# A hybrid attention, state-space and expert layer: a later DRAM copy, a seventh place for expert weights, products that run one pair later, and independent row stores

## The chip, the core and the metric

The kernel runs on one core of one Trainium2 chip. The metric is the time of one execution on the device, in microseconds (us). The program is written with a tile framework: it traces the operations in the order of the source, places the tiles, orders each engine's queue and sets the waits. Engines are PE (matrix multiply; PEld is its weight load), DVE (vector), ACT (activation), POOL (general), and SP, which here only issues DMAs. DMAs are also issued from the queues of ACT and POOL.

## The reference, cut to what matters

512 tokens of width 1024, with 16 learned tokens in front, go through a norm and one wide projection. From it come a latent attention of 16 heads and a state-space scan of 16 heads; both are gated, merged, projected and added to the input. Then follows a mixture of experts: each token chooses one of 4 groups and two of the 8 experts in it.

```
u = rmsnorm(h, norm_mix);  proj = u @ w_in
o_attn = mla_branch(...);  o_ssm = ssd_branch(...)
h = h + (sigmoid(g_attn) * (o_attn @ w_branch_attn)
         + sigmoid(g_ssm) * (o_ssm @ w_branch_ssm)) @ w_out
v = rmsnorm(h, norm_ffn)
for gi in range(4):          # experts of group gi
    hid = silu(v @ w_gate[e]) * (v @ w_up[e])
    out = out + comb[:, e] * (hid @ w_down[e])
return rmsnorm(h + out, norm_final)[16:]
```

An expert has 2 MB of gate and up weights and 1 MB of down weights; 32 experts make 96 MB.

## The kernel before, in words

**Start.** The rows of x are loaded in blocks of 128 (`load_x`), normed and transposed into a split pair `uh`, `ul`. Inside one `in_order` block the queues of ACT, DVE, POOL, PE and SP keep the order of the source: `u_rstd(4)` (line 188) needs the last 16 rows, tile `xm` (line 160), and stands on ACT ahead of the scaling (line 207) that the transposes of block 2 on PE (line 212) need.

**Row buffer.** `vd` is a DRAM buffer of 1024 rows of 1025 words. Its lower 512 rows get the output of the first half of the layer with a scale in the last word (lines 1158 and 1190); the expert stage gathers its token rows from there. The upper 512 rows are a copy of x, with one word more per row (lines 948 and 949): a stand-in that the expert stage's overflow code writes over. The copy depends on nothing, so the framework is free to put its two DMAs anywhere on SP's queue.

**Attention.** In the part around line 950, `load_w` loads the chunks of `wbs` (line 225); `prep` sends rows of the rotated queries to the tiles `qs` by small DMAs on SP (line 798); `find_max` (line 809) multiplies `qs` by `kq` on PE, tile `sp`.

**Routing.** Each token's experts are chosen, and with one-hot products each expert gets a list of up to 64 rows. If an expert had more, `tc.If(over > 0)` (line 1431) would run a slow loop; on these inputs its body does not run, but every engine passes the branch. On the false side SP's queue waits until every DMA that was issued on it has landed.

**Expert stage.** 16 pairs of experts, one expert on each half of the partitions. A pair p does:

```
expert_gu(p)             # gate and up, tanh, products: gu, th, hp
load_gu(...)             # next weights into the places just read
turn_x(p + 1)            # transposes of the next pair's rows (pxT)
combine(p - 1, 1, (0,))  # one-hot product (pc), a quarter
expert_h(p)              # transposes of hp (phT), copy hT by ACT
combine(p - 1, 1, (1,))
y_start; y_mm; y_split   # down product y, split into yh, yl
combine(p, 0)            # two quarters of this pair's one-hot products
```

All this is inside `in_order(act, dve, pe, pool, nc.sync)`, so each queue keeps the order of the source. `combine` adds a pair's rows, for column half hh and row block b, into one of four PSUM sums; after four pairs `add`, `norm` and `scale` (lines 1630 to 1640) finish a group's rows, which `group_rows` gathered into the tiles `res`, and `put_rows` (line 1426) stores them by an indirect DMA on POOL. The framework treats two such stores as writes to the same output, so the second waits until the first has landed. `group_tables` (lines 1598 to 1600) builds on DVE the one-hot tables from which `group_places` (line 1607, PE) finds the group lists; it stands in pair 0 behind the transposes of pair 1.

**Places.** Gate and up weights of expert e lie in place e % 6 (`GU_AT`), down weights in place e % 7. Experts 0 to 5 are loaded as memory comes free, experts 2p + 6 and 2p + 7 (line 1037) when pair p has read its own; line 1046 loads the down weights. The tile `h2`, which holds the output of the first half, is dead once its rows are in `vd`; its memory (tag "v") is then `fin`: two row buffers `res` and the final gain, which is loaded at line 1423. `fence` (line 1488) is a small DMA that SP issues when POOL has issued the first three gathers; down weights 5 and 6 are queued behind it.

Of the kernel before, what the change touches and what calls it, by code (L numbers as in the profile page):

```python
# [9 lines left out]
F32 = mybir.dt.float32  # L10
# [5 lines left out]
ALU = mybir.AluOpType  # L16
# [3 lines left out]
T = 512  # L20
NM = 16
L = T + NM
D = 1024
# [49 lines left out]
def hybrid_layer(ctx: ExitStack, tc, A, out):  # L73
    nc = tc.nc
# [872 lines left out]
    vd = drp.tile([2 * T, D + 1], F32, name="vd")  # L947
    nc.sync.dma_start(vd[T:, :D], A["x"])
    nc.sync.dma_start(vd[T:, D:], A["x"][:, :1])
    PP, pos, l8s, lis = {}, {}, {}, {}  # L950
# [68 lines left out]

    GU_AT = "uu" + "0" + "a" + "d" + "b"  # L1020
    DN_AT = "0aadcee"

    def load_gu(e, parts=(0, 1)):

        if e >= NE:
            return
        i = e % NR
        w = GU_AT[i]
        if i in gus:
            pass  # L1030
        elif w == "u":
            gus[i] = btile(f"gu{i}", n=T)
        else:
            gus[i] = mws[w].tile([128, 4096], F32, tag=f"gu{i}", name=f"gu{i}", bufs=1).rearrange("p (k n) -> p k n", k=KD)
        for h in parts:
            k = slice(h * 4, h * 4 + 4)
            nc.sync.dma_start(gus[i][:, k], A["moe_gu"][e].rearrange("p (k n) -> p k n", k=KD)[:, k])
# [298 lines left out]
    with in_order(pe):  # L1336
# [5 lines left out]
        mws["d"] = ctx.enter_context(tc.tile_pool(name="mwd", bufs=1, reuse_waits="tile", side="right"))  # L1342
        load_gu(4)
        for i in range(3, ND):
# [52 lines left out]
    for x in xgs:  # L1397
        pool.memset(x, 0.0)
    load_gu(5)
    with tc.issue_after(last_rs[0].ins):  # L1400
        for i in range(3, ND):
            if DN_AT[i] == "c":
                load_dn(i)


    fin = btile("fin", n=T, tag="v").rearrange("p k n -> p (k n)")
    res, gfin = [fin[:, b * (D + 1):(b + 1) * (D + 1)] for b in range(2)], fin[:, 2 * D + 2:3 * D + 2]

# [6 lines left out]
    with in_order(pool):  # L1415
        for p in range(NX):
            gather(p)
        pool.memset(flag, 0.0)
        for x in res:
            pool.memset(x, 0.0)  # L1420
    iot = rx.tile([128, 360], F32, tag="rx", name="iot")[:, :GCAP]
    nc.sync.dma_start(iot, bcast_row(A["iota"], GCAP))
    nc.sync.dma_start(gfin, bcast_row(A["g_fin"], D))

    def put_rows(places, rows):
        nc.gpsimd.indirect_dma_start(out=out, out_offset=bass.IndirectOffsetOnAxis(ap=places, axis=0),
                                     in_=rows, in_offset=None, bounds_check=T - 1, oob_is_err=False)


    over = nc.values_load(ovi[0:1, 0:1], min_val=0, max_val=1)  # L1430
    with tc.If(over > 0), tc.tile_pool(name="fb", bufs=1, side="right") as fb:
        wrd = drp.tile([NE, 128, 4], F32, name="wrd")
        nc.sync.dma_start(wrd.rearrange("e p b -> p e b"), wrest)
        for b in range(4):
# [40 lines left out]

            yo = ev.tile([128, D], F32, tag="yl", name="yo", bufs=1)
            fs, fi = fb.tile([128, 2], F32, tag="fs", name="fs"), fb.tile([128, 1], I32, tag="fi", name="fi")
            act.activation(yo, acc, AF.Square, scale=D ** -0.5, accum_out=fs[:, 0:1])
            dve.tensor_scalar(fs[:, 1:2], fs[:, 0:1], EPS, None, op0=ALU.add)
            pool.tensor_tensor(fs[:, 1:2], fs[:, 1:2], mhalf[:, :1], op=ALU.pow)  # L1480
            dve.scalar_tensor_tensor(yo, acc, fs[:, 1:2], gfin, op0=ALU.mult, op1=ALU.mult)
            dve.scalar_tensor_tensor(fs[:, 0:1], gk[:, b:b + 1], GCAP - 0.5, tok1[:, b:b + 1], op0=ALU.is_gt, op1=ALU.mult)
# [3 lines left out]
    mws["e"] = ctx.enter_context(tc.tile_pool(name="mwe", bufs=1, reuse_waits="tile", side="right"))  # L1486
    fence = drp.tile([128, 1], F32, name="fence")
    with tc.issue_after(nc.sync.dma_start(fence, flag).ins):
        for i in range(3, ND):
            if DN_AT[i] == "e":  # L1490
                load_dn(i)

# [22 lines left out]
    def expert_gu(p):  # L1515

        nf = 1 if p < 15 else 2
        gu = [ps("gu") for _ in range(nf)]
        th, hp = (ev.tile([128, 256], F32, tag=x, name=x, bufs=n) for x, n in (("th", 1), ("hp", 2)))
        h_[p] = hp  # L1520
        n = 256 // nf
        for kh in range(2):
            for f in range(nf):
                for k in range(kh * 4, kh * 4 + 4):
                    for e in range(2):
                        r, w = slice(e * 64, (e + 1) * 64), gus[(2 * p + e) % NR][:, k]
                        if nf > 1:
                            w = w.rearrange("p (g f n) -> p g f n", g=2, f=nf)[:, :, f]
                        pe.matmul(gu[f][r, :2 * n], xT[p][:, k, r], w, start=(k == 0), stop=(k == KD - 1), skip_group_check=True)  # L1529
                if kh:  # L1530
                    c = slice(f * n, (f + 1) * n)
                    act.activation(th[:, c], gu[f][:, :n], AF.Tanh, scale=rsl[:, p:p + 1])  # L1532
                    dve.scalar_tensor_tensor(hp[:, c], th[:, c], 1.0, gu[f][:, :n], op0=ALU.add, op1=ALU.mult)  # L1533
                    dve.tensor_mul(hp[:, c], hp[:, c], gu[f][:, n:2 * n])
# [75 lines left out]
    def group_lists():  # L1610
# [6 lines left out]
        dve.tensor_add(gsrc, gw[:, :, 0], gw[:, :, 1])  # L1617

    def group_rows(g):
        for b in range(2):  # L1620
            nc.gpsimd.indirect_dma_start(out=res[b], out_offset=None, in_=vd,
                                         in_offset=bass.IndirectOffsetOnAxis(ap=gsrc[:, b, g:g + 1], axis=0),
                                         bounds_check=2 * T - 1, oob_is_err=False)
# [14 lines left out]
    def scale(g, b):  # L1638
        x = res[b][:, :D]
        dve.scalar_tensor_tensor(x, x, fq[:, 8 + b:9 + b], gfin, op0=ALU.mult, op1=ALU.mult)  # L1640
        put_rows(gdst[:, b, g:g + 1], x)
# [3 lines left out]
    with in_order(act, dve, pe, pool, nc.sync):  # L1645
        for hh in range(2):
            turn_x(0, hh)
        for p in range(16):
            g, last = p // 4, p % 4 == 3
            expert_gu(p)  # L1650
            for h in range(2):
                for e in range(2 * p + NR, 2 * p + NR + 2):
                    load_gu(e, (h,))
            if p < 15:
                turn_x(p + 1, 0)
                turn_x(p + 1, 1)
                if p == 0:
                    group_tables()
                if p:
                    combine(p - 1, 1, (0,))  # L1660
                expert_h(p)
                if p == 0:
                    group_places()
                if p:
                    combine(p - 1, 1, (1,))
                y_start(p)
                for hh in range(2):
# [3 lines left out]
                    if p and p % 4 == 0:  # L1671
                        add(hh, 1)
            else:
                y_start(p)
                expert_h(p, (0,))
                combine(p - 1, 1, (0,))
# [15 lines left out]
            if p < 15:  # L1692
                combine(p, 0)
            if last and p < 15:
                for b in range(2):
                    add(b, 0)
            if p and p % 4 == 0:
# [4 lines left out]
            if p % 4 == 2:  # L1702
                group_rows(g)
        for hh in range(2):
            for b in range(2):
                combine(15, hh, (b,))
                add(b, hh)
                if hh:
                    norm(b)
        for b in range(2):  # L1710
            scale(3, b)
# [117 lines left out]
```

## Time and profile before

| | |
|---|---|
| median of 3 runs | 840.69 us (840.56 to 842.31) |
| the profiled execution | 844.1 us |
| its span, first to last instruction | 842.3 us |
| PE busy in the span | 783.6 us (93%) |
| DVE, ACT, POOL busy | 441.7, 281.9, 162.6 us |
| moved by DMA | 167.58 MB |

The expert stage begins at about 589 us, when the first gathered rows have landed. The rows below give a start in us from the beginning of the span and a duration in us; the square bracket is the time that the engine sat idle before the row and what ended it.

### The profile page before, as it was taken

To read this page: it belongs to the slowest core of one execution; us is meant where nothing else is said; L and a number is where in the kernel's file an instruction comes from. 1 tells how busy PE (TensorE), PEld (TensorE's weight loads), DVE (VectorE), ACT (ScalarE), POOL (GpSimd) and SP (SyncE) were. 2 spreads that over 40 slices of the span, in tenths; PEclk is the share of its full clock that TensorE was granted. 3 is DMA by queue.
4 is the path that set the end of the run, shared out by engine and by line. 5 is a ranking of instruction groups with operands and counts; after the bars stand their busy time and mean duration, and the time that the engine had idled before them with its cause. 6 is when DMAs were issued, how large, how long until landed. Compare 5 with 4: busy or idle time off the path is not lost.

```text
span 842.3 us, 11392 instructions
## 1 busy us (share of the span) xinstructions
PE 783.6 (93%) x4202; PEld 531.0 (63%) x4202; DVE 441.7 (52%) x1005; ACT 281.9 (33%) x541; POOL 162.6 (19%) x222
## 2 busy tenths in 40 slices
PE   4799999999999999999999899995899999999992
PEld 3699988677778878876666588884333333333341
DVE  3487627886465445477774675435223433423423
ACT  4545524433234473155554233311111212212212
POOL 4200011333201000014444200007101121220202
PEclk9899999999999999999999999997799999999997
DMA  9322125234212215020112494586799999999970
GB/s 302 103 101 100 57 97 170 105 126 139 88 63 100 100 36 192 21 60 26 47 52 73 149 420 189 176 333 220 242 421 419 418 418 417 419 420 416 422 284 18
DMA packets 42573, 167.58 MB, mean 199 GB/s; under 512 B 10336, under 2 KB 14832, under 8 KB 26384
## 3 DMA queue, kind: packets, MB, share of 16 engines
q1 hardware_dynamic: 36560, 156.55, 48.8%
q0 software_dynamic: 5136, 10.04, 3.8%
q8 instruction: 35, 0.57, 0.3%
q14 instruction: 26, 0.21, 0.1%
q10 hardware_dynamic: 816, 0.20, 0.1%
HBM read 165.60 MB, written 8.45 MB: 207 GB/s over the span
## 4 chain that ended last, share of the span: by engine, by line
PE 81%; DMA 6%; DVE 6%; ACT 4%; issue 2%; POOL 0%; POOLq 0%; ACTq 0%; SPq 0%; DVEq 0%
PE gu L1529 14%; PE y L1562 7%; PE pbr L671 3%; PE pbr L669 3%; PE pbr L668 3%; PE po L871 2%; DMA xm<-in_x_dram 2%; PE pc L1583 2%; PE ga L241 2%; PE gs L241 2%; PE ga L243 2%; PE ga L242 2%; PE gs L242 2%; PE pout L1092 2%; PE gs L243 2%
## 5 line engine op out<-in xcount | busy, mean ns | idle before, releaser
L1529 PE MATMUL gu<-gu,xT 128*64 128x512 f32 (+1 forms) x544 | 115.5, 578 | 0.0
L1529 PEld LDWEIGHTS gu<-gu,xT 128*64 128x64 f32 x544 | 38.1, 139 | 69.6 <-issue 65.4
L1562 PE MATMUL y<-dn,hT 128*64 128x512 f32 x256 | 60.4, 614 | 0.9
L1533 DVE SCALAR_TENSOR_TENSOR hp<-th,gu 128x256 f32<-128x256 f32 (+1 forms) x17 | 6.9, 405 | 95.5 <-ACT th L1532 95.5
L1570 DVE SCALAR_TENSOR_TENSOR yl<-y,wsl,yh 128x512 fp32r<-128x512 f32 x30 | 22.5, 751 | 50.6 <-ACT yh L1569 49.6
L1532 ACT ACTIVATE th<-gu,rsl 128x256 f32<-128x256 f32 (+1 forms) x17 | 7.8, 461 | 114.7 <-PE gu L1529 114.7
L817 DVE CUSTOM_DVE_ANT_0 sp<-sp,amask 128x144 f32<-128x144 f32 (+4 forms) x80 | 33.9, 459 | 18.0 <-PE sp L809 15.9
L1562 PEld LDWEIGHTS y<-dn,hT 128*64 128x64 f32 x256 | 17.3, 139 | 35.7 <-issue 27.9
L1410 POOL DMA_INDIRECT xg<-vd,idx x16 | 16.4, 1028 | 116.9 <-issue 52.3
L1569 ACT ACTIVATE yh<-y,wsl 128x512 fp32r<-128x512 f32 x30 | 20.6, 685 | 47.1 <-PE y L1562 38.7
L847 PE MATMUL st<-qs,kq 97*128 97x512 f32 (+4 forms) x80 | 28.7, 358 | 1.0 <-DVE kq L792 1.0
L1583 PE MATMUL pc<-yh,st 128*128 128x512 f32 x60 | 27.7, 462 | 0.0
L301 POOL TENSOR_TENSOR rfs<-rfm,mhalf 128x4 f32<-128x4 f32 (+1 forms) x5 | 7.6, 1519 | 92.6 <-DVE rfm L300 92.6
L1503 PEld LDWEIGHTS pxT<-cst,xg 128*128 128x128 f32 x128 | 14.4, 146 | 17.5 <-issue 12.2
L877 POOL TENSOR_TENSOR pw<-pw 128x400 f32<-128x400 f32 x14 | 15.9, 1157 | 44.4 <-PE po L871 44.4
L1505 DVE TENSOR_TENSOR xT<-pxT,pv 128x512 f32<-128x512 f32 x32 | 20.6, 683 | 6.2 <-PE pxT L1503 6.1
L848 PE MATMUL st<-qs,kq 97*128 97x512 f32 (+4 forms) x80 | 23.6, 296 | 0.2 <-DMA qs<-rs 0.2
L1583 PE MATMUL pc<-yl,st 128*128 128x512 f32 x60 | 23.7, 396 | 0.0
L1503 PE MATMUL pxT<-cst,xg 128*128 128x128 f32 x128 | 18.3, 289 | 5.2 <-DMA xg<-vd,idx 5.2
L387 DVE SCALAR_TENSOR_TENSOR cacc<-xp,cwh,cacc 128x528 f32<-128x528 f32 x30 | 22.9, 763 | 0.4
L856 ACT ACTIVATE pw<-st 128x512 f32<-128x512 f32 (+1 forms) x32 | 16.7, 546 | 19.2 <-PE st L852 16.1
L849 PE MATMUL st<-qs,kq 97*128 97x512 f32 (+4 forms) x80 | 23.0, 294 | 0.0
(926 smaller groups left out, 2110.0 us busy)
## 6 DMA issues: line engine op xcount, KB each, us to landing
gu<-in_moe_gu_dram SPq DMA_DIRECT2D x64, 1024.0 KB
dn<-in_moe_dn_dram SPq DMA_DIRECT2D x30, 1024.0 KB
win<-in_win_dram SPq DMA_DIRECT2D x19, 1024.0 KB
lm<-acd SPq DMA_DIRECT2D x16, 256.0 KB
wbs<-in_wbs_dram SPq DMA_DIRECT2D x4, 1024.0 KB
wba<-in_wba_dram SPq DMA_DIRECT2D x4, 1024.0 KB
wo<-in_wout_dram SPq DMA_DIRECT2D x4, 1024.0 KB
vd<-in_x_dram SPq DMA_DIRECT2D x1, 2048.0 KB
```

What stands on the lines that cost most here:

```text
L241: pe.matmul(dst, ah, bh, start=(i == 0), stop=False)
L242: pe.matmul(dst, ah, bl, start=False, stop=False)
L243: pe.matmul(dst, al, bh, start=False, stop=(i == n - 1))
L668: pe.matmul(pb_, wh[:, k], oh[k], start=(k == 0), stop=False)
L669: pe.matmul(pb_, wh[:, k], ol[k], start=False, stop=False)
L671: pe.matmul(pb_, wl[:, k], oh[k], start=False, stop=(k == last))
L817: dve.tensor_tensor_reduce(s_, s_, amask[:, L - nk + n0:L - nk + n1], 1.0, -3.0e38, op0=ALU.add, op1=ALU.max, accum_out=mx[:, n_:n_ + 1])
L847: pe.matmul(d_, kh_[0:97, kb], qh_[0:97, q0:q1], start=True, stop=False)
L1503: pe.transpose(pt[:, k * 128:(k + 1) * 128], xgs[p % NX][:, (hh * 4 + k) * 128:(hh * 4 + k + 1) * 128], ident)
L1529: pe.matmul(gu[f][r, :2 * n], xT[p][:, k, r], w, start=(k == 0), stop=(k == KD - 1), skip_group_check=True)
L1562: pe.matmul(yp[hh][e * 64:(e + 1) * 64], hT_[p][:, f, e * 64:(e + 1) * 64], dns[(2 * p + e) % ND][:, f, hh * 512:(hh + 1) * 512], start=(f ...
L1583: pe.matmul(sums[b, hh], st[:, b * 128:(b + 1) * 128], x[:, c], start=(n == 0 and p % 4 == 0), stop=(n == 1 and p % 4 == 3), skip_group_ch ...
```

## The change

Four things are done. The copy of x into the upper half of `vd` is put behind the last `load_w` before it, which is the last chunk of `wbs`. Expert 4's gate and up weights get a seventh place of their own, in the memory of `h2`, and are loaded behind `fence`; experts 5 and 6 take the places that 4 and 5 had, and pair 2 starts one load instead of two; `fin` is made, and the gain loaded, at the end of pair 2, and the clearing of `res` on POOL is dropped. Of a pair's four one-hot products three run in the next pair, one of them ahead of `expert_h`; `group_tables` comes before pair 0, and the last group finishes block 1 before block 0. Stores of rows no longer wait for each other.

```diff
-    nc.sync.dma_start(vd[T:, :D], A["x"])
-    nc.sync.dma_start(vd[T:, D:], A["x"][:, :1])
+    with tc.issue_after(last_load[0].ins):
+        nc.sync.dma_start(vd[T:, :D], A["x"])
+        nc.sync.dma_start(vd[T:, D:], A["x"][:, :1])
...
-    GU_AT = "uu" + "0" + "a" + "d" + "b"
+    GU_AT = "uu" + "0" + "a" + "d" + "b" + "v"
+    EV = 4
+    def place_of(e):
+        return NR if e == EV else (e - (e > EV)) % NR
...
-        load_gu(4)
+        load_gu(5)
...
-    load_gu(5)
+    load_gu(6)
...
-    fin = btile("fin", n=T, tag="v").rearrange("p k n -> p (k n)")
-    res, gfin = [fin[:, b * (D + 1):(b + 1) * (D + 1)] for b in range(2)], fin[:, 2 * D + 2:3 * D + 2]
...
-        for x in res:
-            pool.memset(x, 0.0)
+    fence = drp.tile([128, 1], F32, name="fence")
+    with tc.issue_after(nc.sync.dma_start(fence, flag).ins):
+        load_gu(EV)
...
-    nc.sync.dma_start(gfin, bcast_row(A["g_fin"], D))
+    stores = []
     def put_rows(places, rows):
+        i = nc.gpsimd.indirect_dma_start(out=out, ...).ins
+        for j in stores:
+            tc.declare_no_dep(i, j, reason="rows of other tokens")
+        stores.append(i)
...
     mws["e"] = ctx.enter_context(tc.tile_pool(name="mwe", bufs=1, reuse_waits="tile", side="right"))
-    fence = drp.tile([128, 1], F32, name="fence")
-    with tc.issue_after(nc.sync.dma_start(fence, flag).ins):
-        for i in range(3, ND):
+    for i in range(3, ND):
...
     def group_rows(g):
+        if g == 0:
+            fin = btile("fin", n=T, tag="v").rearrange("p k n -> p (k n)")
+            res.extend([...])
+            nc.sync.dma_start(res[2], bcast_row(A["g_fin"], D))
...
+        group_tables()
         for p in range(16):
             expert_gu(p)
             for h in range(2):
-                for e in range(2 * p + NR, 2 * p + NR + 2):
-                    load_gu(e, (h,))
+                for e in (2 * p, 2 * p + 1):
+                    if e != EV:
+                        load_gu(e + NR + (e < EV), (h,))
             if p < 15:
                 turn_x(p + 1, 0)
                 turn_x(p + 1, 1)
-                if p == 0:
-                    group_tables()
                 if p:
+                    combine(p - 1, 0, (1,))
                     combine(p - 1, 1, (0,))
                 expert_h(p)
...
                     if p and p % 4 == 0:
-                        add(hh, 1)
+                        for b, h in ([(1, 1)] if hh else [(1, 0), (0, 1)]):
+                            add(b, h)
             else:
                 y_start(p)
+                combine(p - 1, 0, (1,))
                 expert_h(p, (0,))
...
-                combine(p, 0)
-            if last and p < 15:
-                for b in range(2):
-                    add(b, 0)
+                combine(p, 0, (0,))
+            if p % 4 == 3 and p < 15:
+                add(0, 0)
...
-        for hh in range(2):
-            for b in range(2):
+        for b in (1, 0):
+            for hh in range(2):
                 combine(15, hh, (b,))
                 add(b, hh)
-                if hh:
-                    norm(b)
-        for b in range(2):
+            norm(b)
             scale(3, b)
```

The overflow code loads the final gain for itself, since `fin` does not exist there any more; it does not run on these inputs.

## Rows read from the trace of the kernel before

**Rows 1.** The page: DMA share in 40 slices; the chain that ended last, by engine.

```profile
DMA  9322125234212215020112494586799999999970
...
PE 81%; DMA 6%; DVE 6%; ACT 4%; issue 2%; POOL 0%; POOLq 0%; ACTq 0%; SPq 0%; DVEq 0%
```

**Rows 2.** Timeline of SP's queue, first 12 us: start, duration, issue.

```profile
3.74 0.64 SPq L948 DMA_DIRECT2D vd<-in_x_dram  x1
...
5.34 6.51 SPq L160 DMA_DIRECT2D xm<-in_x_dram  x2
```

**Rows 3.** Windows at the start: busy us by engine, PE clock, DMA share, GB/s.

```profile
0.00:14.00 14.00, 4.01 (x16) 3.00 (x16) 4.77 (x11) 7.22 (x12) 6.21 (x12) 1.00 0.87 315
14.00:24.00 10.00, 5.68 (x25) 5.20 (x24) 2.70 (x4) 1.71 (x3) 3.18 (x6) 1.00 1.04 274
27.00:31.00 4.00, 3.98 (x19) 3.99 (x20) 2.45 (x2) 3.81 (x6) 3.50 (x12) 0.50 0.05 11
```

**Rows 4.** Timelines of ACT and PE at the start.

```profile
23.84 0.63 ACT L188 ACTIVATE junk<-xm 16x512 bf16<-16x512 f32 x1 [8.06 <-DMA xm<-in_x_dram]
...
19.41 1.91 PE L321 MATMUL first0a<-uh,win0l 128*128 128x256 f32 x8
27.02 1.97 PE L212 MATMUL pt<-cst,xin 128*128 128x128 f32 x8 [5.70 <-ACT xin L207]
```

**Rows 5.** SP's queue around 325 us; the products that read qs (min/median/max ns, first to last).

```profile
322.37 0.53 SPq L225 DMA_DIRECT2D wbs<-in_wbs_dram  x1
327.32 1.60 SPq L798 DMA_DIRECT2D qs<-rs  x2
...
L809 PE MATMUL sp<-kq,qs x80: 170/334/495, 344.2 to 445.7; 96*128 96x144 f32 x16, 96*128 96x272 f32 x16, 96*128 96x16 f32 x16, 96*128 96x400 f32 x16
```

**Rows 6.** Timeline of pair 0, from the copy of hT to the down product.

```profile
602.12 0.38 ACT L1545 ACTIVATE hT<-phT 128x256 f32<-128x256 f32 x1 [1.44 <-PE phT L1543]
...
604.30 0.34 PE L1607 MATMUL pg<-gtab,rrg 128*128 128x8 bf16 x8 [2.22 <-DVE gtab L1600]
...
604.58 5.35 PE L1562 MATMUL y<-dn,hT 128*64 128x512 f32 x16
```

**Rows 7.** Timeline of PE in a regular pair.

```profile
697.33 7.09 PE L1529 MATMUL gu<-gu,xT 128*64 128x512 f32 x32
...
706.07 0.41 PE L1543 MATMUL phT<-cst,hp 128*128 128x128 f32 x2 [0.17 <-DVE hp L1534]
...
707.01 3.65 PE L1562 MATMUL y<-dn,hT 128*64 128x512 f32 x16
...
711.74 7.09 PE L1529 MATMUL gu<-gu,xT 128*64 128x512 f32 x32
```

**Rows 8.** SP's queue at the branch.

```profile
588.45 0.34 SPq L1488 DMA_DIRECT2D fence<-flag  x1
597.78 1.01 SPq L1046 DMA_DIRECT2D dn<-in_moe_dn_dram  x2
```

**Rows 9.** Windows in the expert stage, columns as in rows 3.

```profile
588.00:594.00 6.00, 5.05 (x16) 2.58 (x18) 1.57 (x4) 0.00 (x0) 3.58 (x7) 0.50 0.34 69
610.00:800.00 190.00, 186.99 (x872) 73.26 (x874) 68.86 (x148) 37.70 (x77) 32.39 (x29) 1.00 1.02 419
812.00:818.00 6.00, 6.00 (x55) 3.83 (x55) 0.75 (x1) 0.18 (x2) 0.00 (x0) 1.00 0.57 212
818.00:820.00 2.00, 2.00 (x19) 1.16 (x15) 0.58 (x2) 0.69 (x3) 0.00 (x0) 1.00 0.04 15
```

**Rows 10.** Timelines of PE, DVE and POOL in the last 21 us.

```profile
821.57 2.79 PE L1562 MATMUL y<-dn,hT 128*64 128x512 f32 x12
...
831.83 1.29 DVE L1640 SCALAR_TENSOR_TENSOR fin<-fin,fq 128x1024 f32<-128x1024 f32 x1 [0.44 <-POOL fq L1636]
...
831.98 2.07 POOL L1426 DMA_INDIRECT out_dram<-fin,gdst  x1 [0.18 <-issue]
837.12 0.98 POOL L1426 DMA_INDIRECT out_dram<-fin,gdst  x1 [3.07 <-DMA out_dram<-fin,gdst]
```

More of the change, by code (lines that the diff above doesn't have):

```diff
@@ L1026, in load_gu @@
             return
-        i = e % NR
+        i = place_of(e)
         w = GU_AT[i]
@@ L1030, in load_gu @@
             pass
-        elif w == "u":
-            gus[i] = btile(f"gu{i}", n=T)
+        elif w in "uv":
+            gus[i] = btile(f"gu{i}", n=T, tag=w)
         else:
@@ L1418, in hybrid_layer @@
         pool.memset(flag, 0.0)
-        for x in res:
-            pool.memset(x, 0.0)
+    fence = drp.tile([128, 1], F32, name="fence")
+    with tc.issue_after(nc.sync.dma_start(fence, flag).ins):
+        load_gu(EV)
     iot = rx.tile([128, 360], F32, tag="rx", name="iot")[:, :GCAP]
     nc.sync.dma_start(iot, bcast_row(A["iota"], GCAP))
-    nc.sync.dma_start(gfin, bcast_row(A["g_fin"], D))
+    stores = []
     def put_rows(places, rows):
-        nc.gpsimd.indirect_dma_start(out=out, out_offset=bass.IndirectOffsetOnAxis(ap=places, axis=0),
-                                     in_=rows, in_offset=None, bounds_check=T - 1, oob_is_err=False)
+        i = nc.gpsimd.indirect_dma_start(out=out, out_offset=bass.IndirectOffsetOnAxis(ap=places, axis=0),
+                                         in_=rows, in_offset=None, bounds_check=T - 1, oob_is_err=False).ins
+        for j in stores:
+            tc.declare_no_dep(i, j, reason="rows of other tokens")
+        stores.append(i)
     over = nc.values_load(ovi[0:1, 0:1], min_val=0, max_val=1)
@@ L1474, in hybrid_layer @@
             nc.sync.dma_start(vd[T + b * 128:T + (b + 1) * 128, :D], acc)
-            yo = ev.tile([128, D], F32, tag="yl", name="yo", bufs=1)
+            yo, go = ev.tile([128, D], F32, tag="yl", name="yo", bufs=1), fb.tile([128, D], F32, tag="fw", name="go", bufs=3)
+            nc.sync.dma_start(go, bcast_row(A["g_fin"], D))
             fs, fi = fb.tile([128, 2], F32, tag="fs", name="fs"), fb.tile([128, 1], I32, tag="fi", name="fi")
@@ L1480, in hybrid_layer @@
             pool.tensor_tensor(fs[:, 1:2], fs[:, 1:2], mhalf[:, :1], op=ALU.pow)
[L1481 removed]
+            dve.scalar_tensor_tensor(yo, acc, fs[:, 1:2], go, op0=ALU.mult, op1=ALU.mult)
             dve.scalar_tensor_tensor(fs[:, 0:1], gk[:, b:b + 1], GCAP - 0.5, tok1[:, b:b + 1], op0=ALU.is_gt, op1=ALU.mult)
@@ L1486, in hybrid_layer @@
     mws["e"] = ctx.enter_context(tc.tile_pool(name="mwe", bufs=1, reuse_waits="tile", side="right"))
-    fence = drp.tile([128, 1], F32, name="fence")
-    with tc.issue_after(nc.sync.dma_start(fence, flag).ins):
-        for i in range(3, ND):
-            if DN_AT[i] == "e":
-                load_dn(i)
+    for i in range(3, ND):
+        if DN_AT[i] == "e":
+            load_dn(i)
     xT, h_, y_ = {}, {}, {}
@@ L1525, in expert_gu @@
                     for e in range(2):
-                        r, w = slice(e * 64, (e + 1) * 64), gus[(2 * p + e) % NR][:, k]
+                        r, w = slice(e * 64, (e + 1) * 64), gus[place_of(2 * p + e)][:, k]
                         if nf > 1:
@@ L1617, in group_lists @@
         dve.tensor_add(gsrc, gw[:, :, 0], gw[:, :, 1])
+    res = []
     def group_rows(g):
+        if g == 0:
+            fin = btile("fin", n=T, tag="v").rearrange("p k n -> p (k n)")
+            res.extend([*(fin[:, b * (D + 1):(b + 1) * (D + 1)] for b in range(2)), fin[:, 2 * D + 2:3 * D + 2]])
+            nc.sync.dma_start(res[2], bcast_row(A["g_fin"], D))
         for b in range(2):
@@ L1639, in scale @@
         x = res[b][:, :D]
-        dve.scalar_tensor_tensor(x, x, fq[:, 8 + b:9 + b], gfin, op0=ALU.mult, op1=ALU.mult)
+        dve.scalar_tensor_tensor(x, x, fq[:, 8 + b:9 + b], res[2], op0=ALU.mult, op1=ALU.mult)
         put_rows(gdst[:, b, g:g + 1], x)
@@ L1647, in hybrid_layer @@
             turn_x(0, hh)
+        group_tables()
         for p in range(16):
-            g, last = p // 4, p % 4 == 3
+            g = p // 4
             expert_gu(p)
             for h in range(2):
-                for e in range(2 * p + NR, 2 * p + NR + 2):
-                    load_gu(e, (h,))
+                for e in (2 * p, 2 * p + 1):
+                    if e != EV:
+                        load_gu(e + NR + (e < EV), (h,))
             if p < 15:
@@ L1663, in hybrid_layer @@
                     group_places()
-                if p:
+                else:
                     combine(p - 1, 1, (1,))
```

## The prediction

> **What bounds the kernel now.** I read the chain of waits first: PE carries 81% of it, and no other engine more than 6% [rows 1]. So a saving counts where PE sits idle or runs slowly, and at the two ends. The DMA line of the slices says where transfers may take over: it stands at 9 in the first slice and again from the thirtieth to the thirty-eighth, the expert stage [rows 1].
>
> The timelines then show the places. At the start PE ends its first product at 21.3 (19.41 + 1.91) and waits 5.70 us for ACT [rows 4]. ACT in turn waits 8.06 us for `xm`, until 23.84 [rows 4], though SP began to issue `xm` at 5.34 [rows 2]. In front of it on SP's queue stands the 2 MB copy of x, issued at 3.74 [rows 2]. [...] In pair 0 PE waits 2.22 us for the group tables, and the down product behind that wait takes 5.35 us [rows 6], where the same 16 matmuls take 3.65 us in a regular pair [rows 7]. A regular pair lasts 14.41 us (711.74 - 697.33), with one wait on its path, 0.17 us before the transposes of hp [rows 7]. At the end the second store waits 3.07 us for the first [rows 10].
>
> The sum is made against the profiled execution, 844.1 us (span 842.3, 1.8 around it); the median of the runs, 840.69, lies 3.4 us (0.4%) lower. About 0.2%, 1.7 us, is what a measurement of this kernel can tell from no change.
>
> **The change, part by part.**
>
> *The copy leaves the start: -8.0 us.* Ahead of `xm` remain 1.5 MB of x, 0.5 MB of gain, 0.1 MB of small loads and two chunks of 1 MB: with 1.05 MB to the chunk, 4.2 MB. At 315 GB/s the queues had moved 4.4 MB by 14 us [rows 3], so `xm` and the fourth block (0.5 MB, 1.6 us at that rate) would be in by about 16 to 17. From the arrival of `xm` to PE's next transpose ACT and POOL need 3.2 us (27.02 - 23.84) [rows 4]: 20.2, before PE ends its product at 21.3. So the whole 5.70 us goes. With no wait I expect no fall of the clock either: 4.0 us at 0.50 [rows 3] do 2.0 us of work, and with the shoulders of the slow stretch I take 2.3. Bounds: -5.0 if `xm` comes 2 us later than reckoned and the clock still falls in part, -8.5.
>
> *The copy in its new place: 0.* It brings two DMAs to SP's queue behind the chunk at 322.37 [rows 5]. Passed by it are the row DMAs `qs` at 327.32 [rows 5]. The copy took about 8 us of the DMA engines (2.1 MB at 274 GB/s) [rows 3]; behind 2.5 us of the chunk it would end near 334, the rows land a little later, and the first product that reads them starts at 344.2 [rows 5]. That slack of some 9 us is the cover; PE works on `wbs` meanwhile. Without cover it would cost up to 8 us and 2 us of slow clock. The column of 512 single words has no price of its own in the trace; in the first place both DMAs together fit between 14 and 24 [rows 3], so 10 us bounds the pair, and nothing suggests less than 0.
>
> *Group tables ahead of pair 0: -3.7 us.* Their six DVE operations move to where DVE idles while PE does the first gate product. The down product can then start when hT is copied, at 602.5 (602.12 + 0.38), plus some 0.06, instead of 604.58: 2.0 us [rows 6]. Kept warm, it takes 3.65 instead of 5.35: 1.7 us [rows 6, 7]. Bounds -2.0 and -4.2.
>
> *Products one pair later: -2.4 us.* PE does the same products; the one that moves ahead of the transposes of hp (two matmuls) fills the wait of 0.17 us [rows 7], in 14 pairs. Bounds: 0, if the wait only moves to hT, and -3.4, if the shorter block at the end of the pair saves another 0.07 each time.
>
> *Seventh place, fence and branch: +1.5 us.* The weights stream without a pause from about 598: DMA share 1.02 at 419 GB/s [rows 9]. A pair's 6 MB (6.29 million bytes) take 15.0 us at that rate, PE needs 14.41: the lead shrinks all the way. The stream drains between 812 and 818 [rows 9]; the last down weights are needed at 821.57 [rows 10]. So the slack is about 3.5 us, and it decides what the gains above are worth, since PE now comes 3.7 + 2.4 = 6.1 us earlier, at 815.5. The new place takes one expert's 2.1 MB (5.0 us) out of the stream and into the gap between 588 and 594, where only 69 GB/s are moved [rows 9]; the gain row (0.5 MB, 1.25 us) enters the stream: -3.75 us. Against that, SP must pass the branch. Between the fence at 588.45 and the first load behind the branch at 597.78 lie 9.3 us [rows 8]. Now two issues stand in between (0.8 us), and on the false side SP waits until they have landed, about 5 us, part of it beside the passage of the branch. Queued behind are down weights 5 and 6 and experts 7 and 8. I take 2.7 us of delay (bounds 0.8 and 5.3): the stream ends at 818 - 3.75 + 2.7 = 817.0, 1.5 us after the need. Bounds 0 and +4.0. The value lies nearer the lower, since the fence too had to land there.
>
> *Independent stores, last group by blocks: -2.6 us.* The second store starts at 837.12 though its rows were scaled at 833.1 (831.83 + 1.29) [rows 10]: 3.8 us with the 0.18 of issue. The new order gives back one scaling, 1.29 us, as the adds of block 0 stand on DVE behind the scaling of block 1. Bounds -1.0 and -3.8.
>
> *At nothing:* the dropped clearing of `res` and the gain's new issue (POOL and SP wait for nothing there), `fin` made at the end of pair 2, two pairs before its use, and the stores of the first three groups, behind which POOL's gathers have pairs of lead.
>
> Sum: -8.0 + 0 - 3.7 - 2.4 + 1.5 - 2.6 = -15.2 us: 828.9 for a profiled execution, **825.5 us** for the median.
>
> **The rivals.**
>
> *The branch holds the loads in full.* If SP passes the branch only after expert 4 has landed, the whole 5 us is added, and the stream ends 4.0 us after PE's need instead of 1.5: 828.0 us. For it speaks that 9.3 us pass at the branch with DMA nearly idle [rows 8, 9]; against it that most of the landing lies beside that time. [...] Chance 0.14.
>
> *The copy collides in attention.* If the framework puts it later than 322, or its words take long, the rows `qs` come late and PE stands for 8 us and then runs slowly: +10, 835.5 us. Against it: 9 us of slack [rows 5]. Chance 0.07.
>
> *The copy was not what held `xm`.* If `xm` waits for the weight chunks alone, the change does not do at the start what it says, and -8.0 goes: 833.5 us. Against it: 274 GB/s for 10 us after 14 us, when 4.4 MB had already been moved [rows 3]. Chance 0.06.
>
> *Slower: SP sticks at the branch.* The price is the time until the first load behind it. Every microsecond beyond 2.7 is paid by PE at the last down weights, so from a first load at about 617 (597.8 + 2.7 + 15.2 + 1.7, before's clock) the kernel is slower; at 620 it takes 843 us. It would need more than twice the 9.3 us of rows 8; the only thing for it is that this pause is not explained by what DMA moves meanwhile [rows 9]. Chance 0.04.
>
> **How the numbers follow.** The forecast keeps 0.69. Its best bounds sum to -8.5 - 4.2 - 3.4 - 3.8 = -19.9 (820.8), its worst are not met together. The range 819.5 to 833.5 holds the forecast, the first rival and the edge of the third, and leaves out the collision, the sticking branch and some tail: under 0.2. Of both signs only the sticking branch matters: slower by over 0.2% 0.03, the same 0.01, faster 0.96.
>
> **What would show it.** Right: `xm` used at 16 to 18 us, PE without a wait of over 1 us before 30 and at clock 1.00; the copy's DMAs on SP after the last chunk of `wbs` and no wait of PE before the first `sp`; the down product of pair 0 at 3.65 us; pairs of 14.2 us; the first load behind the branch 11 to 13 us after the fence; a wait of 0 to 3 us in pair 15 for down weights; the last store some 2.6 us earlier against the end of the last down product. Wrong: a wait for `xm` that stays, an idle PE between 315 and 340, or a long wait for weights in any pair.

## The result and the profile after

The changed kernel takes 832.49 us (median of 4 runs, 831.86 to 833.65), the kernel before in the same series 841.50 (840.56 to 842.31): ratio 0.9895, interval 0.9877 to 0.9913. It is 9.0 us faster. Forecast were 15.2 us less; the time lies 7 us above the forecast and 1 us under the upper end of the range. The profiled execution has a span of 830.1 us.

The page of the changed kernel, DMA share in slices and the chain that ended last:

```profile
DMA  7322225334322137111122685667799999999980
...
PE 72%; DMA 13%; issue 5%; DVE 4%; ACT 3%; POOL 1%; POOLq 0%; SPq 0%; ACTq 0%; DVEq 0%
```

Against [rows 1] the first slice fell from 9 to 7, and a DMA share of 13% came into the chain, where 6% had stood. That is the whole story in two lines: the start was relieved, and the weight stream took over in the expert stage.

**The start.** Timelines of SP and PE:

```profile
3.42 1.38 SPq L160 DMA_DIRECT2D xm<-in_x_dram  x2
...
25.12 1.09 PE L212 MATMUL pt<-cst,xin 128*128 128x128 f32 x8
26.46 0.77 PE L321 MATMUL first0b<-uh,win0h 128*128 128x272 f32 x4 [0.25 <-ACT uh L174]
```

`xm` is issued in 1.38 us instead of 6.51 [rows 2], the transposes that took 1.97 us at a granted clock of 0.50 [rows 3] take 1.09 at 1.00, and the wait of 5.70 us in front of them [rows 4] is gone. The product `first0b`, which began at 35.01 us before, begins at 26.46.

**Pair 0 and a regular pair.** Timeline of PE at the down product of pair 0; then in pair 6:

```profile
588.94 3.65 PE L1569 MATMUL y<-dn,hT 128*64 128x512 f32 x16 [0.29 <-ACT hT L1552]
```

```profile
663.38 7.09 PE L1536 MATMUL gu<-gu,xT 128*64 128x512 f32 x32
...
671.57 0.39 PE L1590 MATMUL pc<-yl,st 128*128 128x512 f32 x1
671.80 0.40 PE L1590 MATMUL pc<-yh,st 128*128 128x512 f32 x1
672.03 0.39 PE L1590 MATMUL pc<-yl,st 128*128 128x512 f32 x1
672.26 0.38 PE L1550 MATMUL phT<-cst,hp 128*128 128x128 f32 x2
...
677.42 1.08 PE L1536 MATMUL gu<-gu,xT 128*64 128x512 f32 x4
```

The down product of pair 0 waits for the copy of hT alone, 0.29 us, and takes 3.65 us at a granted clock of 1.00, not 5.35 [rows 6] at 0.68. A pair lasts 14.04 us (677.42 - 663.38) instead of 14.41 [rows 7]. From gate product to gate product pair 0 takes 14.73 us (593.18 - 578.45) instead of 20.11 (610.99 - 590.88). Both gains are there, and larger than forecast; run 7 shows how much of pair 0's is owed to the tables.

**Where they went.** SP's queue at the branch, then PE's gate products from pair 9 on:

```profile
576.02 0.34 SPq L1422 DMA_DIRECT2D fence<-flag  x1
576.54 12.92 SPq L1043 DMA_DIRECT2D gu<-in_moe_gu_dram  x2
589.78 0.89 SPq L1052 DMA_DIRECT2D dn<-in_moe_dn_dram  x2
```

```profile
705.50 7.72 PE L1536 MATMUL gu<-gu,xT 128*64 128x512 f32 x32
720.16 4.51 PE L1536 MATMUL gu<-gu,xT 128*64 128x512 f32 x18
726.40 3.65 PE L1536 MATMUL gu<-gu,xT 128*64 128x512 f32 x14 [1.73 <-DMA gu<-in_moe_gu_dram]
737.00 4.50 PE L1536 MATMUL gu<-gu,xT 128*64 128x512 f32 x18
742.32 3.65 PE L1536 MATMUL gu<-gu,xT 128*64 128x512 f32 x14 [0.82 <-DMA gu<-in_moe_gu_dram]
752.92 4.97 PE L1536 MATMUL gu<-gu,xT 128*64 128x512 f32 x18
759.33 3.65 PE L1536 MATMUL gu<-gu,xT 128*64 128x512 f32 x14 [1.44 <-DMA gu<-in_moe_gu_dram]
769.93 7.99 PE L1536 MATMUL gu<-gu,xT 128*64 128x512 f32 x32
784.86 4.69 PE L1536 MATMUL gu<-gu,xT 128*64 128x512 f32 x18
791.14 3.65 PE L1536 MATMUL gu<-gu,xT 128*64 128x512 f32 x14 [1.59 <-DMA gu<-in_moe_gu_dram]
```

The two issues of expert 4 stretch over 12.92 us: the program as built has the branch between its two halves. SP goes on at about 589.1 (576.54 + 12.92 less an issue of 0.4), 13.1 us after the fence, where it was 9.33 [rows 8]. From pair 9 on PE stands for the second halves of gate and up weights. Measured from start to end against 7.09 us, the gate products of pairs 9 to 14 take 0.6 + 2.8 + 1.9 + 3.0 + 0.9 + 2.8 = 12.0 us too long (pair 10: 726.40 + 3.65 - 720.16 = 9.89). The waits in brackets show less than half of that; the rest has no mark of its own in the profile, as in pairs 9 and 13, whose products are too long without a bracket.

**The end.** Timelines of PE, DVE and POOL:

```profile
811.34 1.08 PE L1569 MATMUL y<-dn,hT 128*64 128x512 f32 x4
...
818.58 1.29 DVE L1654 SCALAR_TENSOR_TENSOR fin<-fin,fq 128x1024 f32<-128x1024 f32 x1 [0.69 <-POOL fq L1650]
819.78 0.68 DVE L1644 TENSOR_TENSOR fin<-fin,pc 128x512 f32<-128x512 f32 x1
...
820.15 1.05 POOL L1431 DMA_INDIRECT out_dram<-fin,gdst  x1 [1.61 <-DVE fin L1654]
824.28 1.03 POOL L1431 DMA_INDIRECT out_dram<-fin,gdst  x1 [1.61 <-DVE fin L1654]
```

Neither store waits for the other any more; each waits for its scaling.

**The balance** of the two profiled spans, cut at the same instructions. "wq" and "wo" are the first issue of the rotary half of the query weights (303.53 and 293.49 us) and of the output weights (498.05 and 485.61).

| stretch | before | after | difference |
|---|---|---|---|
| start to `first0b` | 35.01 | 26.46 | -8.55 |
| to wq | 268.52 | 267.03 | -1.49 |
| to wo | 194.52 | 192.12 | -2.40 |
| to the first gate product | 92.83 | 92.84 | 0.01 |
| to the last down product | 230.69 | 232.89 | +2.20 |
| to the end | 20.73 | 18.76 | -1.97 |

Nothing shows the second and third line to be work of the change. In all fourteen profiled executions of this study the second stretch took either 266.9 to 267.0 or 268.4 to 268.6 us, seven times each, and without the copy at the start both ways; in the pair above the granted clock between 120 and 160 us is 0.96 before and 1.00 after. The third varied from 192.0 to 194.5. So the profiled execution of before was a long one, and 9.0 us, the difference of the medians, is the result.

### The profile page after: what moved, and what is told of

Read it like the earlier page. It is cut to its first block, busy times and chain, and to the rows that moved or that the text cites. A ratio compares the mean times of both kernels' runs of the same rounds, so it can differ in the third digit from the quotient of the medians.

```text
span 830.1 us, 11391 instructions
## 1 busy us (share of the span) xinstructions
PE 779.7 (94%) x4202; PEld 531.6 (64%) x4202; DVE 440.7 (53%) x1005; ACT 281.8 (34%) x541; POOL 159.5 (19%) x220
## 4 chain that ended last, share of the span: by engine, by line
PE 72%; DMA 13%; issue 5%; DVE 4%; ACT 3%; POOL 1%; POOLq 0%; SPq 0%; ACTq 0%; DVEq 0%
DMA gu<-in_moe_gu_dram 8%; PE gu L1536 7%; PE y L1569 4%; PE pbr L668 3%; PE pbr L671 3%; PE pbr L669 3%; PE po L871 2%; PE ga L241 2%; PE gs L241 2%; PE ga L243 2%; PE ga L242 2%; PE gs L242 2%; PE pout L1098 2%; PE gs L243 2%; PE pout L1100 2%
## 5 line engine op out<-in xcount | busy, mean ns | idle before, releaser
L1536 PE MATMUL gu<-gu,xT 128*64 128x512 f32 (+1 forms) x544 | 120.7, 574 | 5.6 <-DMA gu<-in_moe_gu_dram 5.6
L1536 PEld LDWEIGHTS gu<-gu,xT 128*64 128x64 f32 x544 | 41.7, 137 | 76.8 <-issue 59.2
L1569 PE MATMUL y<-dn,hT 128*64 128x512 f32 x256 | 58.7, 599 | 1.2 <-ACT hT L1552 0.3
L1510 PEld LDWEIGHTS pxT<-cst,xg 128*128 128x128 f32 x128 | 14.4, 146 | 17.5 <-issue 17.5
```

Source lines behind the costliest of these rows:

```text
L1510: pe.transpose(pt[:, k * 128:(k + 1) * 128], xgs[p % NX][:, (hh * 4 + k) * 128:(hh * 4 + k + 1) * 128], ident)
L1569: pe.matmul(yp[hh][e * 64:(e + 1) * 64], hT_[p][:, f, e * 64:(e + 1) * 64], dns[(2 * p + e) % ND][:, f, hh * 512:(hh + 1) * 512], start=(f ...
```

## The experiments

Each run is compared with the kernel before in its own series; medians of before were 841.06 (runs 1 to 4), 840.34 (5 to 8) and 839.92 us (9 to 12). The table gives the ratio to before and, of each profiled execution, the stretches of the balance that matter and PE's waits for gate and up weights.

| run | median | ratio, interval | wo to first gate | first gate to last down | to the end | waits |
|---|---|---|---|---|---|---|
| before | | 1 | 92.83 | 230.69 | 20.73 | 0 |
| changed | 832.49 | 0.9895, 0.9877 to 0.9913 | 92.84 | 232.89 | 18.76 | 5.6 |
| 1 copy alone | 831.34 | 0.9896, 0.9873 to 0.9919 | 92.63 | 229.34 | 20.78 | 0 |
| 2 copy left | 841.99 | 1.0007, 0.9990 to 1.0024 | 92.46 | 233.48 | 18.75 | 5.5 |
| 3 expert 4 behind | 830.40 | 0.9877, 0.9852 to 0.9901 | 92.79 | 230.31 | 18.72 | 4.2 |
| 4 no fence | 824.76 | 0.9811, 0.9790 to 0.9833 | 95.39 | 221.39 | 18.80 | 0 |
| 5 old order | 833.42 | 0.9913, 0.9896 to 0.9931 | 92.70 | 233.90 | 18.75 | 3.8 |
| 6 no fence, old order | 830.17 | 0.9878, 0.9859 to 0.9897 | 95.53 | 226.22 | 18.75 | 0 |
| 7 no fence, late tables | 828.25 | 0.9858, 0.9838 to 0.9877 | 95.63 | 225.25 | 18.77 | 0 |
| 8 no fence, dependent stores | 823.45 | 0.9808, 0.9789 to 0.9827 | 95.68 | 221.22 | 18.74 | 0 |
| 9 no fence, six places | 824.71 | 0.9817, 0.9794 to 0.9840 | 92.82 | 224.62 | 18.75 | 1.0 |
| 10 no fence, half ahead | 821.62 | 0.9777, 0.9757 to 0.9797 | 93.44 | 221.70 | 18.77 | 0 |
| 11 no fence, old tail | 823.65 | 0.9803, 0.9784 to 0.9823 | 95.91 | 220.88 | 18.02 | 0 |
| 12 copy alone, no fence | 832.76 | 0.9911, 0.9890 to 0.9931 | 92.87 | 229.79 | 20.73 | 0 |

**1 and 2: the copy by itself.** The theory: the start gives all the gain, and the expert stage gives back what it gains. Run 1 is the kernel before with

```diff
-    nc.sync.dma_start(vd[T:, :D], A["x"])
-    nc.sync.dma_start(vd[T:, D:], A["x"][:, :1])
+    with tc.issue_after(last_load[0].ins):
+        nc.sync.dma_start(vd[T:, :D], A["x"])
+        nc.sync.dma_start(vd[T:, D:], A["x"][:, :1])
```

> The kernel before with the copy of x alone moved behind the last chunk of wbs; all else as before. Theory: the front gives the change nearly all that it gains, and what PE gains in the expert stage is taken back there by the weight stream. Then this kernel takes 841.5 - 8.5 = 833.0 us, within 1 us of the changed kernel's 832.5. The prediction as it stands (front -8.0, the rest -7.2) gives 833.5 here as well, but wants the changed kernel 7 us below it. Rival: the fall of the granted clock at 120 to 160 and 465 to 472 us of the profiled run of before (about 3.9 us in all) comes from the copy too; then 829.5 to 830.

Run 2 is the changed kernel with these lines the old way.

> The changed kernel with the copy of x left at the start. Theory (front nearly everything, expert stage nets about nothing): 832.5 + 8.5 = 841.0 us, no different from before within 1 us. If the parts add up as predicted: 834.5 or so, 7 us below before. Rival (clock of two later stretches also comes from the copy): 844.

Measured: 0.9896 and 1.0007. The copy alone is the whole gain, and all the other edits together make no difference that can be measured. Run 1 came out 1.7 us under its expectation, which lies inside its interval. The rival isn't borne out: the second stretch of the balance took 267.00 us in run 1, but 268.58 in run 3, without the copy, as in run 2, with it; the third took 192.92 in run 1 and 192.88 in run 2.

**3: what SP waits for at the branch.**

```diff
+    load_gu(EV, ())
...
-    with tc.issue_after(nc.sync.dma_start(fence, flag).ins):
-        load_gu(EV)
+    nc.sync.dma_start(fence, flag)
...
+    load_dn(5)
+    with tc.issue_after(last_dn[0].ins):
+        load_gu(EV)
+    load_dn(6)
```

The first line makes the place and loads nothing.

> The changed kernel with expert 4 loaded whole behind the branch, after down weights 5. Theory (SP sits at the branch until the half of expert 4 ahead of it has landed, and the stream binds): the first load behind the branch comes about 9.3 us after the fence as in before, not 13.8; the stream carries one half more (1.05 MB, 2.5 us) and starts some 4 us earlier: 831.0 us, with the same kind of waits for gate and up weights in pairs 10 to 14. Rival 1 (the branch takes its 13 us whatever is under way): first load at 13 us, stream 2.5 us later: 835. Rival 2 (the stream doesn't set the time): 832.5, unchanged.

SP's queue in run 3:

```profile
578.91 0.34 SPq L1424 DMA_DIRECT2D fence<-flag  x1
587.53 0.33 SPq L1053 DMA_DIRECT2D dn<-in_moe_dn_dram  x1
```

With nothing of expert 4 ahead, the first load behind the branch comes 8.6 us after the fence, not 13.1; the time is 830.4 us (expected 831.0). So the half ahead holds SP for 4.5 us more. Loading it there costs more than it brings by the length of the stretch, 230.31 us against 232.89; the ratios of the two kernels overlap.

What SP waits for, at the line of the branch, in before and then in the changed kernel (us in total, times, longest):

```profile
SPq L1431 <- SPq L1431: 8.0, 1, 8.0
```

```profile
SPq L1439 <- SPq L1439: 10.8, 1, 10.8
```

The landing events in the traces (a DMA reports in 16 parts) say what ends these waits. In before the fence's last part landed at 596.88 us and SP went on at 596.90; in run 3 it was 587.12 and 587.13. In run 5, which has the changed kernel's fence and its half ahead, the half landed at 590.95 and SP went on at 590.97; in the changed kernel at 588.04 and 588.52, where the fence had landed by 583.28. So SP waits for the landing, and the fence too is a load to wait for.

The landing explains the waits of before, run 3 and run 5 to within 0.02 us; of the changed kernel the last 0.5 us stay open. In runs 3, 9, 10 and 12 nothing was under way for the first of the landings that SP checks, and from the branch to that check 6.0, 2.8, 5.1 and 3.1 us passed. What fills them no run shows.

**4: the stream's start.**

```diff
-    flag = cp.tile([128, 1], F32, name="flag")
...
-        pool.memset(flag, 0.0)
-    fence = drp.tile([128, 1], F32, name="fence")
-    with tc.issue_after(nc.sync.dma_start(fence, flag).ins):
-        load_gu(EV)
+    load_gu(EV)
```

> The changed kernel without the fence: expert 4 is loaded in both halves as soon as its place is free (about 565 us), and nothing holds SP at POOL's gathers. Theory (late start of the stream is what costs the 12 us of waits in pairs 9 to 14): SP passes the branch at 578 to 582, the first load behind it comes 8 to 11 us earlier than 589.8, the waits for gate and up weights go, 823 us (821 to 826). Rival 1: the gathers of the first pair are held up by the 2 MB, PE starts pair 0 up to 5 us later and gets part of it back: 828 to 830. Rival 2 (the waits come from the new order of the products, not from the stream's start): 832.5.

SP's queue and PE's first transposes in run 4:

```profile
569.75 0.81 SPq L1043 DMA_DIRECT2D gu<-in_moe_gu_dram  x2
579.64 0.96 SPq L1052 DMA_DIRECT2D dn<-in_moe_dn_dram  x2
```

```profile
579.58 1.94 PE L1506 MATMUL pxT<-cst,xg 128*128 128x128 f32 x8 [7.76 <-DMA xg<-vd,idx]
```

What SP's queue waits for, in the changed kernel and then in run 4 (us in total, times, longest):

```profile
SPq L1052 <- DMA gu<-in_moe_gu_dram: 54.2, 24, 3.3
SPq L1043 <- DMA dn<-in_moe_dn_dram: 53.4, 22, 3.5
SPq L1043 <- DMA gu<-in_moe_gu_dram: 50.3, 21, 3.4
```

```profile
SPq L1043 <- PE gu L1532: 43.7, 15, 6.0
SPq L1052 <- PE y L1565: 35.0, 7, 6.0
```

824.8 us. The loads behind the branch start 9.5 us earlier (579.64 against 589.1), the waits of pairs 9 to 14 are gone (every gate product from pair 1 to 14 takes 7.09 us), and the two largest groups of SP's waits, 78.7 us in all, are now for PE to free places. In the changed kernel the three largest, 157.9 us, are for earlier loads; in run 4 these three come to 89.8 us. Between first gate and last down product 11.5 us are saved. 2.6 us of them are paid before: expert 4's 2 MB run into the first gathers, for which PE now waits 7.76 us, as rival 1 had it.

**5 and 6: the order of the products, with and without the stream in the way.** Both have, against the changed kernel and run 4,

```diff
-                    combine(p - 1, 0, (1,))
                     combine(p - 1, 1, (0,))
                 expert_h(p)
...
-                combine(p, 0, (0,))
-            if p % 4 == 3 and p < 15:
-                add(0, 0)
+                combine(p, 0)
+            if p % 4 == 3 and p < 15:
+                for b in range(2):
+                    add(b, 0)
```

> The changed kernel with the one-hot products and their adds in the old order (two of the four in the next pair), the last group by blocks as changed. Theory (the stream sets the time of the expert stage): pairs come at 14.4 us again, the waits for gate and up weights shrink by as much, and the time stays at 832.5, at most 1 us above. Rival (the shorter pairs count in full): 14 pairs of 0.35 us more, 837.4.

> The kernel without the fence, with the one-hot products and adds in the old order. There SP waits for PE to free the places, and PE never for weights. Theory: now the order counts in full, 14 times 0.35 = 4.9 us: 824.8 + 4.9 = 829.7. Rival (the order is worth only the removed wait of 0.17 us, as predicted): 827.2. Rival 2 (the stream still binds): 825 to 826.

833.4 us in run 5: pairs of 14.4 us again, and 0.9 us lost by the medians, 1.0 in the stretch; the ratios overlap, so this is not clear of noise. In run 6 the same edit costs 4.8 us between first gate and last down product (226.22 against 221.39), and 0.0067 of the time (5.6 us) by the ratios. The gain is real, and the changed kernel could not use it.

Why 0.35 us a pair, when the idle row [rows 7] shows 0.17? Products of PE in a pair of before, ahead of the transposes of hp:

```profile
705.51 0.39 PE L1583 MATMUL pc<-yl,st 128*128 128x512 f32 x1
706.07 0.41 PE L1543 MATMUL phT<-cst,hp 128*128 128x128 f32 x2 [0.17 <-DVE hp L1534]
```

In the pair of the changed kernel shown above such products follow each other at 0.23 us (671.57, 671.80, 672.03, 672.26), though each lasts 0.39. After 705.51 the next could have begun at 705.74; it began at 706.07, 0.33 us later. The idle time counts only from the end of the one before.

**7: the group tables.**

```diff
-        group_tables()
         for p in range(16):
...
                 turn_x(p + 1, 1)
+                if p == 0:
+                    group_tables()
```

> The kernel without the fence, with the group tables built in pair 0 behind the transposes of pair 1, as before the change. Theory (PE sets the time here): what the trace of the changed kernel showed for pair 0, 5.4 us, comes back: 830.2; the prediction's 3.7 us would give 828.5. Rival (the first pair is hidden by something else): 825.

828.25 us: 3.9 us in the stretch (225.25 against 221.39) and 0.0047 (4.0 us) by the ratios. Expected was 5.4, with the changed kernel's pair 0 as measure; that had taken in 1.2 us of its gate product (7.92 us at a granted clock of 0.89 instead of 9.12 at 0.77), which the tables don't set. The prediction's 3.7 was the better number.

**8 and 11: the tail.** Run 8 takes away `declare_no_dep` and keeps the order by blocks:

```diff
-        for j in stores:
-            tc.declare_no_dep(i, j, reason="rows of other tokens")
```

> The kernel without the fence, with the stores of the output rows depending on each other again. In the changed kernel the two last stores stand 4.1 us apart by the order of the blocks, while before the second one came 5.1 us after the first. Theory: independence is worth 1.0 us beside the order by blocks: 825.8. Rival (independence carries nearly all of the predicted 2.6): 827. Rival 2 (the first three groups' stores also hold up POOL's gathers and with them PE): over 828.

Run 11 keeps the independent stores and has the old order:

```diff
-        for b in (1, 0):
-            for hh in range(2):
+        for hh in range(2):
+            for b in range(2):
                 combine(15, hh, (b,))
                 add(b, hh)
-            norm(b)
-            scale(3, b)
+                if hh:
+                    norm(b)
+        for b in range(2):
+            scale(3, b)
```

> The kernel without the fence, with the last group again by halves of the row (both blocks of a half, then the other half), the stores still independent. With dependent stores and the order by blocks the time had not changed, so the order alone should carry the 2.0 us between the last down product and the end (18.75 us with it, 20.75 without). Theory: the end takes 1.3 to 2.0 us longer, 826 to 826.8. Rival (either of the two is enough, since independent stores let the second follow at once): 825.

Stores of run 11:

```profile
813.70 2.07 POOL L1427 DMA_INDIRECT out_dram<-fin,gdst  x1 [0.18 <-issue]
816.07 0.98 POOL L1427 DMA_INDIRECT out_dram<-fin,gdst  x1 [0.30 <-issue]
```

Both expectations missed. From last down product to end: 20.73 us with neither edit, 18.74 with the order alone, 18.02 with independence alone, 18.8 with both. With the order by blocks the scalings stand 4.1 us apart and the second store has nothing to wait for; independence then adds nothing. With independence alone the second store follows 2.4 us after the first; the order by blocks on top takes 0.7 us back, since the adds of block 0 stand behind the scaling of block 1 (819.78 behind 818.58 above).

**9 and 10: the seventh place.** Run 9 is run 4 with the six places of before (`place_of(e)` is `e % 6`); run 10 has one half of expert 4 ahead of the branch and the other behind down weights 5:

```diff
-    load_gu(EV)
+    load_gu(EV, (0,))
...
+    load_dn(5)
+    with tc.issue_after(last_dn[0].ins):
+        load_gu(EV, (1,))
+    load_dn(6)
```

> The changed kernel without the fence and with six places for gate and up weights (expert 4 again in the sixth order of before, the seventh place unused until fin). Theory (the stream's start decides, and its bytes): the first gathers are no longer held up by expert 4, so pair 0 starts 2.6 us earlier than without the fence alone, while the stream carries 2.1 MB more behind the branch (5.0 us): some 4 us of waits for gate and up weights come back in the last pairs, 826 us (825 to 828). Rival 1 (the stream has that much slack): 822. Rival 2 (without the place the gain of the missing fence is lost): 830 to 832.

> The kernel without the fence, with only the first half of expert 4 ahead of the branch and the second half behind down weights 5. Theory: the first gathers are held up by 1 MB instead of 2, so pair 0 starts 1.3 us earlier; the stream carries 1 MB more (2.5 us), of which at most 1.5 us show as waits: 824 us (823 to 826), no clear difference from the whole ahead (824.8). Rival (the hold of the gathers has nothing to do with expert 4): 826.

PE's first transposes and its one marked wait for weights in run 9:

```profile
577.01 1.94 PE L1504 MATMUL pxT<-cst,xg 128*128 128x128 f32 x8 [5.16 <-DMA xg<-vd,idx]
...
783.34 3.65 PE L1530 MATMUL gu<-gu,xT 128*64 128x512 f32 x14 [0.97 <-DMA gu<-in_moe_gu_dram]
```

Run 9: 824.7 us. Without the place the stage is 3.2 us longer (224.62 against 221.39), and the first gathers come 2.6 us sooner: the place filled whole ahead of the branch is worth nothing. Run 10, with half of it, has 93.44 and 221.70, so nearly both advantages, and takes 821.6 us, the lowest median here (2.2% under before), though its interval meets those of runs 4, 8, 9 and 11. That no wait came back was not expected: the stream bore the second half behind the branch (1.05 MB, 2.5 us at 419 GB/s) without any.

**12: the same fence in the old kernel.** Run 1 without its fence.

> The kernel before with the copy moved alone, and without its fence. There PE's pairs take 14.4 us and no pair waits for weights. Theory (the start of the stream counts only once PE has come nearer to it): 831.3, unchanged within 0.8 us. Rival (the fence or the passage of the branch also costs time of itself): 3 us or more less.

832.8 us, no gain. Where PE takes 14.4 us a pair, the start of the stream was worth nothing (ratio 0.9911, with the fence 0.9896 in run 1). The fence only began to cost when the other edits had brought PE nearer to its weights.

## Why the prediction was right and wrong

*The copy leaves the start (-8.0): right.* -8.55 at `first0b`, with `xm` in time and no stretch at 0.50 (the granted clock is 1.00 from 14 to 35 us); -9.7 us by the medians of run 1, with an interval that reaches from -6.8 to -10.7.

*The copy in its new place (0): right.* It is issued at 312.87 us behind the last chunk, and no product waits there in the profile.

*Group tables (-3.7): right by itself.* 3.9 us in run 7.

*Products one pair later (-2.4): mis-sized by half.* 4.8 us in run 6. The step took the idle time of 0.17 us for what a late product costs; by the starts it is 0.33. Even the bound of -3.4 was too small.

*Stores and tail (-2.6): nearly right, and for one reason of two.* -1.97. Independence alone brings 2.7 where the step had 3.8, and the order by blocks takes back 0.7 where it had 1.3; that this order would do nearly as much without independence was not seen.

*Seventh place, fence and branch (+1.5): the step that failed.* In its place stood about +11.5 within the stage, by run 4 against the changed kernel (by the medians run 4 gains 7.7, since its first gathers come later). Three things were wrong in it. First, the slack was read at one consumer, the last: "the last down weights are needed at 821.57 [rows 10]. So the slack is about 3.5 us". The down weights were never late, and pair 15 doesn't wait. The first to come late are second halves of gate and up weights in pairs 9 to 14. SP's loads of experts 20 and 21, in before and in the changed kernel, with the chain of the changed kernel (start, length, what):

```profile
704.83 8.16 SPq L1037 DMA_DIRECT2D gu<-in_moe_gu_dram  x4
```

```profile
696.50 7.78 SPq L1043 DMA_DIRECT2D gu<-in_moe_gu_dram  x4
```

```profile
680.99 22.89 DMA gu<-in_moe_gu_dram
703.95 22.41 DMA gu<-in_moe_gu_dram
726.40 3.65 PE gu L1536 x14
```

In this chain a load needed some 22.4 us from issue to use. By this estimate, in before the last of these four was out at 712.99, so in at about 735.4, and PE wanted it half way through the gate product of pair 10, 740.55 + 3.5 = 744.1: 8.7 us of slack, which the profile of before would have given (its landing events give 734.45, so 9.6). After the change PE wants it, counted from the fence, 8.0 us earlier (723.7 - 576.02 against 744.1 - 588.45), and SP issues it 3.7 us later (704.28 - 576.02 against 712.99 - 588.45): 3.0 us short, and pair 10 is 2.8 us too long.

Second, the delay at the branch was 3.8 us (13.1 against 9.33) where the step took 2.7 of bounds 0.8 to 5.3. It took the lower side, since the fence too had to land there; but the half landed 4.8 us after the fence (588.04 against 583.28). The first rival, that the branch holds the loads, was the right mechanism with a chance of 0.14; run 3 and the landing events bear it out. Its price, 4.0 us at the end of the stream, was read from the same wrong place. And the second half of expert 4 stood behind the branch, where the step had both ahead.

Third, of what PE gains the step let the stream take back 1.5 us, and it took all: what PE gained in pair 0 and in the pairs (3.9 + 4.8 us) went into waiting, and the stretch became 2.2 us longer. Runs 5 and 6 show it: the same edit is worth 1.0 us of the stretch behind the late stream and 4.8 without it.

The forecast of a faster kernel held, and the range held, because the one term that needed no stream was large and right. That the time still lies inside the range is in part luck: its upper end, 833.5, was set by a wait for `xm` that stays, and the rival that was right in kind was priced at 828.0. The other rivals, a collision of the copy in attention, a wait for `xm` that stays and a kernel made slower by the branch, did not come about.

Three slips in the working changed nothing: 3.8 less 1.29 is 2.5, not 2.6; a first load at 620 us makes 845 us by the step's own rule, not 843; and the DMA line of [rows 1] stands at 9 in the 24th slice too.

## What to carry to other kernels

Read the slack of a stream at every consumer that waits for it, from issue plus landing to need, and not at its last byte: here the end had 3.5 us and the middle 8.7, and the middle gave way first, since what PE gains per pair and what SP loses at the branch both fall due there. Price each edit on the kernel in which the others are already made: the same order of products was worth 4.8 us of the stage with the stream free and 1.0, not clear of noise, behind it, and the same fence nothing in the old kernel and 7 to 8 us in the new (0.9811 against 0.9895). In this kernel, where SP waits at the branch for all that it has issued, a load put ahead of the branch is also a wait for all that stands behind it, a fence of 512 bytes (8.0 us at the branch in before) no less than a load of 1 MB (10.8 us in the changed kernel).

## What the runs showed of the hardware

Three things had not been expected. The idle time behind a chain of matmuls understated what it cost, 0.17 us against 0.33, as told above. A load held up the gathers of the first pair: 2 MB ahead of 0.5 MB gathers moved PE's start by 2.6 us (95.39 us from wo in run 4, 92.82 in run 9). And behind the fence the DMA engines were busy and moved next to nothing. Windows of the changed kernel, then of run 4 (busy us by engine, PE clock, DMA share, GB/s):

```profile
578.00:580.00 2.00, 2.00 (x7) 0.59 (x7) 1.89 (x7) 0.00 (x0) 0.00 (x0) 0.50 1.55 74
580.00:582.00 2.00, 2.00 (x12) 0.65 (x10) 0.65 (x4) 0.00 (x0) 1.20 (x1) 0.96 0.75 45
582.00:584.00 2.00, 2.00 (x12) 0.62 (x10) 0.00 (x0) 0.00 (x0) 0.00 (x0) 1.00 0.68 41
```

```profile
572.00:574.00 2.00, 0.00 (x0) 0.00 (x0) 0.12 (x2) 0.00 (x0) 1.26 (x2) 0.50 0.90 360
574.00:576.00 2.00, 0.00 (x0) 0.00 (x0) 0.00 (x0) 0.00 (x0) 1.81 (x3) 0.50 1.04 426
```

For 6 us the first half of expert 4 hardly moves (74 to 41 GB/s at shares of 0.68 to 1.55). In run 4 SP stands at the branch as well, from 570.56 to 579.64, and expert 4's 2 MB move at 360 to 426 GB/s meanwhile. So the branch alone does not do it. The fence's own DMA, 128 single words to DRAM, is under way in the slow stretch: by the landing events it took 7.0 to 8.4 us from issue to last landing in the six kernels that have it (before, changed, runs 1, 2, 3 and 5). Whether it slows the load was not tried by itself; a fence of one word would be the next experiment.
